# A decoder step on one core: which queue issues the sample's cache pages, when the mixer's output weights are converted, and where the attention output is split

## The chip, the cores and the metric

The kernel runs on one core of a Trainium2 chip. The metric is device time in microseconds (us) of one execution, the median of several runs; lower is better. The engines are TensorE (PE in the rows, its weight loads PEld), VectorE (DVE), ScalarE (ACT), GpSimd (POOL) and SyncE (SP). SP and POOL issue the transfers here, each from a queue of its own that works in order. Every engine takes its instructions in the order of the program.

## The reference

One layer of a hybrid decoder step for a prompt of 1024 tokens and a sample of 8 sequences with 4 new tokens each. A half-step SwiGLU block, a mixer, and a second half-step SwiGLU block follow each other, each under RMS norm and a modulation by the conditioning vector. The mixer:

```
n = modulated(x, g_mix, 1)
c_q, c_kv, k_pe, u, v, g_a, g_b = split_in(n @ w_in)
...
o_lat = attend(q_lat, q_pe, kv, k_pe)              # prompt: causal; sample: over the paged cache
o_a = einsum('bshc,chv->bshv', o_lat, w_uv)
v_n = layer_norm(gelu(v), ln_v_g, ln_v_b)
o_b = spatial_gating(gelu(u), v_n, w_s, b_s, chunk_len)
merged = sigmoid(g_a) * (o_a @ w_pa) + sigmoid(g_b) * (o_b @ w_pb)
x = x + gate[:, 1] * (merged @ w_o)
```

For the sample, `attend` reads 32 pages of 128 rows for each of 8 sequences through `page_table`: once for the scores (latent and rope part of each key row) and once for the values.

## The kernel before

Every fp32 product is made of three passes (`mm3`, L324 to L326): each operand is split into a rounded part (`whi`, by a cast on ACT, L186 or L330) and the remainder (`wlo`, by a subtraction on VectorE, L187 or L331). `conv_to` (L172 on) does that for the weights, in the order in which they were planned; `use(i, la)` asks for operand i and converts `la` operands ahead of it. It also brings the weights in through SP (`dma_to`, L163 and L161), some ahead of their conversion. Output weights w_o have one step more: POOL multiplies them by the gate first (`wg`, L184).

The prompt is worked in two halves of 512 tokens. After the first SwiGLU block and the projections of queries and keys, the mixer attends (about 905 to 1113 us) and then runs `post` for the one half (to about 1399) and the other (to about 1690). `post` splits the attention output `oaT` into OA (four casts, four subtractions), then takes v's rows (`rows_b` over four operands), u's rows, and five rounds p = 0 to 4. A round takes, for f = 0 and 1, the gates ga and gb (24 matmuls each), the output product `down` of the round before (with the two w_o operands, f = 0 only), and the merge weights pab, which meet OA and OB. In the plan of a round the operands stand in the order ga0, gb0, o0, o1, pab0, ga1, gb1, pab1. `ev_v`, a generator that is stepped between the matmuls, turns v's rows into normalised ones: four gelus on ACT, then squares, then VectorE's scaling.

The sample's attention (`s_attn`) is a generator too, stepped between the prompt's matmuls from about 891 to 1360. It works on four sequences at a time (g = 0, then 1). For g it makes 16 steps of scores: step r needs two pages of each of the four sequences (tiles pk, eight pages; `load_pk` asks for those of step r + 1 when step r is due; the matmuls of L1589 go through the four sequences first). Then follow eight groups of values (matmuls of L1635): each takes four tiles nat, one for each of the chunks c, with one page of each sequence, and asks for chunk c + 4 when chunk c has been used. A page is one transfer of 144 KB (pk) or 128 KB (nat), whose address comes from the page table, so its issue takes a few register instructions (L1546) ahead of the transfer (L1547). In both loads the pages alternate between SP and POOL. The pages are issued where the generator asks for them, so they share SP's queue with the weights, the x rows (L1078) and the stores, and POOL's with wg, the parts of norms that POOL does (L518, L519), and the product xT (L565). Tiles come from a pool of 46 slots (`u`); a load waits until its slot's former reader is done.

Of the kernel before, what the change touches and what calls it, by code (L numbers as in the profile page):

```python
# [9 lines left out]
FR = mybir.dt.float32r  # L10
# [6 lines left out]
P = 128  # L17
# [70 lines left out]
class Step:  # L88
# [1219 lines left out]

    def post(self, e, hf, nT, after=None, on=lambda what, p=0: None):
        nc = self.nc  # L1310
        OA = []
        for kt in range(4):
            w = self.u([P, 2, 512], FR, name="oa")
            self.split(w[:, 0], w[:, 1], self.oaT[kt // 2][hf][:, kt % 2])
            OA.append(w)

        vn = [self.u([P, 4, 256], F32, name="vn") for _ in range(2)]
        ub = [self.u([P, 4, 256], F32, name="ub") for _ in range(2)]
# [23 lines left out]
        def ev_u(ps):  # L1342
            for t in range(4):
                for g in range(2):
                    nc.scalar.activation(out=ub[g][:, t], in_=ps[t][:, 256 * g:256 * g + 256], func=AF.Gelu_apprx_tanh)
# [11 lines left out]
        fv.step()  # L1357
        self.fillers.append(fv)
        on("v")
        ps = [self.psb() for _ in range(3)] + [self.psa()]  # L1360
        ev_u(self.rows_b(e["u"], nT, ps))
        fv.finish()
# [22 lines left out]
        for p in range(5):  # L1385
            d = e["pairs"][p]
            if p < 4:
                hcur = []
                for f in range(2):
                    sg = []  # L1390
                    sgt = self.u([P, 2, 512], F32, name="sg")
                    for n in ("ga", "gb"):
                        ps = self.psa()
                        hi, lo = self.use(d["%s%d" % (n, f)], 2 if n == "gb" and f == 0 and p else 1)
                        for k in range(8):
                            x = nT[k]
                            self.mm3(ps, (hi[:, k, :], lo[:, k, :]), (x[:, 0], x[:, 1]), k == 0, k == 7)
                            if k % 2:
                                self.tick(1.3)
                        t = sgt[:, len(sg)]  # L1400
                        nc.scalar.activation(out=t, in_=ps, func=AF.Sigmoid)
                        sg.append(t)
                        if p == 0 and f == 0:
                            (mix if n == "ga" else mix_T)()
# [3 lines left out]
                    hi, lo = self.use(d["pab%d" % f], 2 if p == 3 and f else 1)  # L1408
                    if f == 0:
                        on("m", p)  # L1410
                    for n, X in ((0, OA), (1, OB)):
                        ps = self.psa()
# [7 lines left out]
                    w = self.u([P, 2, 512], FR, name="mg")  # L1420
# [128 lines left out]
    def s_attn(self):  # L1549

        nc, a = self.nc, self.a
# [7 lines left out]
        def load_pk(g, r, bs=(0, 1, 2, 3)):  # L1559
            if g > 1 or r > 15:  # L1560
                return
            for b in bs:
                t = self.u([96, 2, 3, P], F32, name="pk")
                for i in range(2):
                    self.page(t[:, i], "kvp", "o r c k -> r (o c) k", 4 * g + b, 2 * r + i, (nc.sync, nc.gpsimd)[i])
                pk[g, r, b] = t

        def load_nat(g, i):
            if (g, i) in nat or g > 1 or i > 31:
                return  # L1570
            t = self.u([P, 4, 256], F32, name="nat")
            for b in range(4):
                self.page(t[:, b], "kvn", "o k c -> k (o c)", 4 * g + b, i, (nc.sync, nc.gpsimd)[b % 2])
            nat[g, i] = t

        for g in range(2):
            if g == 0:
                load_pk(g, 0)
# [25 lines left out]
            for i in range(4):  # L1604
                load_nat(g, i)
# [16 lines left out]
            for i4 in range(8):  # L1622
                ps = self.pss()
                for i in range(4):
                    c = 4 * i4 + i
                    nc.tensor.transpose(ps[:, P * i:P * i + P], pt[c // 8][:, P * (c % 8):P * (c % 8) + P], self.idt)
                w = self.u([P, 4, P])
# [3 lines left out]
                for i in range(4):  # L1631
                    c = 4 * i4 + i
                    t = nat.pop((g, c))
# [36 lines left out]
        oa = self.s("sqn", [P, P], F32, 1)  # L1670
# [540 lines left out]
```

## Time and profile before

| | |
|---|---|
| median of 3 runs | 2395.5 us (2390.06 to 2398.54) |
| profiled execution | 2394.01 us |
| its span, first to last instruction | 2392.4 us |
| granted TensorE clock, mean | 0.987 |
| TensorE busy | 2294.7 us (96%) |
| VectorE, ACT, POOL busy | 57%, 34%, 36% |

The span is the time between the first and the last instruction of the profiled execution; 1.6 us of its time lie around it. A row of the timeline holds instructions of one form that follow each other on one engine, merged: start, length, engine, line, operation, tiles, count, and in brackets the idle time ahead of the row with what ended it. SPq and POOLq are the queues of SP and POOL on which transfers are issued; the length of such a row is that of the issue, not of the transfer.

### The profile page before, as it was taken

The numbers are of one execution on the slowest core, as the hardware profiler recorded it, in microseconds if no ns is written. First come the engines' busy times: TensorE is split into PE (matmuls) and PEld (weight loads), VectorE is DVE, ScalarE is ACT, GpSimd is POOL, SyncE is SP. The second block draws the span as 40 slices with busy tenths as digits, with TensorE's granted clock in tenths as the row PEclk, the third lists the DMA queues.
The fourth block names the chain that finished last, engine by engine and source line by source line (L and its number), as shares of the span: only waits on it lengthen the run. The fifth ranks groups of instructions, "written<-read, shape, count | busy, mean of one in ns | idle before, by whom it ended". The sixth has DMA issues, their size and how long they took to land.

```text
span 2392.4 us, 37074 instructions
## 1 busy us (share of the span) xinstructions
PE 2294.7 (96%) x12989; PEld 1750.0 (73%) x12989; DVE 1372.9 (57%) x1897; ACT 819.4 (34%) x1411; POOL 858.0 (36%) x822
## 2 busy tenths in 40 slices
PE   6999999998998999999999999999899999999998
PEld 4678787876776775556677777777677878877876
DVE  3766666663556555674344455445666666666557
ACT  4322222323334244553332243222532223233433
POOL 1364556450125123243223310011156565552125
PEclk9899999999999999999999999999999999999999
DMA  6244444459855237568877725542144444358643
GB/s 264 84 144 139 158 137 150 154 182 383 328 184 184 110 80 220 173 183 227 226 212 217 234 77 194 186 139 83 63 151 151 144 150 152 135 184 305 239 155 142
DMA packets 192516, 420.10 MB, mean 176 GB/s; under 512 B 21981, under 2 KB 80298, under 8 KB 192330
## 3 DMA queue, kind: packets, MB, share of 16 engines
q1 hardware_dynamic: 179242, 381.01, 46.7%
q0 software_dynamic: 12800, 36.19, 5.4%
q8 instruction: 103, 1.69, 0.3%
q14 instruction: 83, 0.68, 0.1%
q10 hardware_dynamic: 288, 0.52, 0.1%
HBM read 337.31 MB, written 78.23 MB: 174 GB/s over the span
## 4 chain that ended last, share of the span: by engine, by line
PE 77%; issue 6%; DMA 5%; DVE 5%; ACT 3%; POOL 2%; POOLq 1%; SPq 1%; DVEq 0%; ACTq 0%
PE psa L324 15%; PE psa L325 15%; PE psa L326 15%; PE psb L324 7%; PE psb L325 7%; PE psb L326 6%; PE pss L622 3%; DVE wlo L187 1%; PE pss L1589 1%; POOLq L1546 1%; PE psa L1211 1%; PE psa L441 1%; DMA nat<-in_kvn 1%; DMA w<-in_w1d 1%; DMA wada<-in_w_ada 1%
## 5 line engine op out<-in xcount | busy, mean ns | idle before, releaser
L187 DVE TENSOR_TENSOR wlo<-w,whi 128x1024 fp32r<-128x1024 f32 (+1 forms) x273 | 304.3, 1153 | 163.5 <-ACT whi L186 138.0
L186 ACT CAST whi<-w 128x1024 fp32r<-128x1024 f32 (+1 forms) x273 | 243.5, 927 | 208.9 <-PE psb L325 61.1
L326 PE MATMUL psa<-xT,ws 128*128 128x512 f32 x800 | 311.7, 390 | 2.0 <-DVE ws L331 2.0
L324 PE MATMUL psa<-xT,ws 128*128 128x512 f32 x800 | 313.2, 391 | 0.0
L325 PE MATMUL psa<-xT,ws 128*128 128x512 f32 x800 | 311.2, 389 | 0.0
L331 DVE TENSOR_TENSOR ws<-wsum,ws 128x512 fp32r<-128x512 f32 x160 | 170.5, 1065 | 28.8 <-ACT ws L330 28.8
L869 POOL TENSOR_TENSOR h<-hf,h 128x512 f32<-128x512 f32 x60 | 97.6, 1627 | 235.7 <-issue 191.0
L326 PEld LDWEIGHTS psa<-xT,ws 128*128 128x128 f32 x800 | 150.1, 188 | 34.3 <-DVE ws L331 2.8
L325 PEld LDWEIGHTS psa<-xT,ws 128*128 128x128 f32 x800 | 150.3, 188 | 30.6
L324 PEld LDWEIGHTS psa<-xT,ws 128*128 128x128 f32 x800 | 150.2, 188 | 30.4
L324 PE MATMUL psa<-xT,whi 128*128 128x512 f32 x384 | 160.1, 417 | 1.6 <-ACT xT L742 1.6
L325 PE MATMUL psa<-xT,whi 128*128 128x512 f32 x384 | 153.0, 398 | 0.0
L326 PE MATMUL psa<-xT,wlo 128*128 128x512 f32 x384 | 152.5, 397 | 0.0
L325 PE MATMUL psa<-wlo,whi 128*128 128x512 f32 x308 | 122.3, 397 | 9.4 <-DVE wlo L187 9.4
L331 DVE TENSOR_TENSOR ws<-w,ws 128x512 fp32r<-128x512 f32 x120 | 111.4, 928 | 33.9 <-ACT ws L330 33.9
L324 PE MATMUL psa<-whi 128*128 128x512 f32 x308 | 123.0, 399 | 6.2 <-ACT whi L186 6.2
L324 PE MATMUL psb<-xT,ws 128*128 128x512 f32 x320 | 127.1, 397 | 0.0
L325 PE MATMUL psb<-xT,ws 128*128 128x512 f32 x320 | 125.1, 391 | 0.0
L326 PE MATMUL psb<-xT,ws 128*128 128x512 f32 x320 | 124.6, 389 | 0.0
L324 PE MATMUL psb<-whi 128*128 128x512 f32 x308 | 122.5, 398 | 0.0
L326 PE MATMUL psa<-whi,wlo 128*128 128x512 f32 x308 | 121.6, 395 | 0.0
L325 PE MATMUL psb<-wlo,whi 128*128 128x512 f32 x308 | 121.2, 393 | 0.0
(397 smaller groups left out, 4820.2 us busy)
## 6 DMA issues: line engine op xcount, KB each, us to landing
wada<-in_w_ada SPq DMA_DIRECT2D x72, 512.0 KB
x<-x SPq DMA_DIRECT2D x40, 512.0 KB
pk<-in_kvp SPq DMA_DIRECT2D x128, 144.0 KB
pk<-in_kvp POOLq DMA_DIRECT2D x128, 144.0 KB, 3.8
w<-w1h SPq DMA_DIRECT2D x35, 512.0 KB
w<-w2h SPq DMA_DIRECT2D x35, 512.0 KB
nat<-in_kvn SPq DMA_DIRECT2D x128, 128.0 KB
nat<-in_kvn POOLq DMA_DIRECT2D x128, 128.0 KB, 3.0
```

What stands on the lines that cost most here:

```text
L186: self.nc.scalar.copy(hv(w.hi), src)
L187: self.nc.vector.tensor_tensor(out=hv(w.lo), in0=src, in1=hv(w.hi), op=ALU.subtract)
L324: nc.tensor.matmul(out, sh, mh, start=first, stop=False, skip_group_check=cont)
L325: nc.tensor.matmul(out, sh, ml, start=False, stop=False, skip_group_check=cont)
L326: nc.tensor.matmul(out, sl, mh, start=False, stop=last, skip_group_check=cont)
L331: self.nc.vector.tensor_tensor(out=lo, in0=src, in1=hi, op=ALU.subtract)
L441: nc.tensor.matmul(ps[32 * k:32 * k + 32, 256 * qq:256 * qq + 256], self.sc[:, 4 * kh + k, :], t[:, k, :], start=(kh == 0), stop=(kh == 1))
L622: self.nc.tensor.matmul(ps[32 * j:32 * j + 32, cols], st[:, k, :], mv, start=(k < 4), stop=(k >= nk - 4))
L869: nc.gpsimd.tensor_tensor(out=g, in0=t, in1=g, op=ALU.mult)
L1211: nc.tensor.matmul(ps[:, c:c + n], q, K[:, c:c + n], start=True, stop=not diag)
L1546: v = eng.value_load(self.pt[0:1, 32 * b + i:32 * b + i + 1], min_val=0, max_val=self.a[name].shape[0] - 1)
L1589: nc.tensor.matmul(ps[32 * b:32 * b + 32, 0:256], self.sqT[:, ch, 4 * g + b, :], ts[b][:, :, ch, :], start=(ch == 0), stop=(ch == 2))
```

## The change

Three edits. In `post` the split of OA moves from the head to the place behind v's rows and the first step of `ev_v`. In the rounds p = 1 to 3, `use` of ga0 (not only of gb0) converts two operands ahead, so that o0 is converted at ga0 and o1 at gb0, where both were converted at gb0. In `load_pk` both pages of the first of the four sequences are issued by SP; in `load_nat` two of the 16 pages of four chunks go from POOL to SP (sequence 3 in the first chunk, sequence 1 in the third, sequences counted from 0). SP issues five of eight pk pages and ten of sixteen nat pages, POOL the rest: 128 and 128 pk pages become 160 and 96, and so do the nat pages.

```
     def post(self, e, hf, nT, after=None, on=lambda what, p=0: None):
         nc = self.nc
-        OA = []
-        for kt in range(4):
-            w = self.u([P, 2, 512], FR, name="oa")
-            self.split(w[:, 0], w[:, 1], self.oaT[kt // 2][hf][:, kt % 2])
-            OA.append(w)
...
         fv.step()
         self.fillers.append(fv)
         on("v")
+        OA = []
+        for kt in range(4):
+            w = self.u([P, 2, 512], FR, name="oa")
+            self.split(w[:, 0], w[:, 1], self.oaT[kt // 2][hf][:, kt % 2])
+            OA.append(w)
...
-                        hi, lo = self.use(d["%s%d" % (n, f)], 2 if n == "gb" and f == 0 and p else 1)
+                        hi, lo = self.use(d["%s%d" % (n, f)], 2 if f == 0 and p else 1)
...
-                    self.page(t[:, i], "kvp", "o r c k -> r (o c) k", 4 * g + b, 2 * r + i, (nc.sync, nc.gpsimd)[i])
+                    self.page(t[:, i], "kvp", "o r c k -> r (o c) k", 4 * g + b, 2 * r + i, (nc.sync, nc.gpsimd)[i and b > 0])
...
-                self.page(t[:, b], "kvn", "o k c -> k (o c)", 4 * g + b, i, (nc.sync, nc.gpsimd)[b % 2])
+                self.page(t[:, b], "kvn", "o k c -> k (o c)", 4 * g + b, i, (nc.sync, nc.gpsimd)[b % 2 and b + i % 4 != 3])
```

The order of TensorE's instructions is the same in both programs. What stands in a row on the others, at three places:

SP's queue in the first half of `post`, at round p = 3, ahead of the load of the first of its two w_o operands (`in_w_o`; `sx` holds the page table), the difference:

```order
+L1546 TENSOR_LOAD sx
+L1546 ISA x2
+L1547 ISA
+L1547 DMA nat<-in_kvn 128x256
 L163 DMA w<-in_w_o 128x1024
+L1546 TENSOR_LOAD sx
```

A page that POOL issued before now stands directly ahead of the load, and another directly behind it; each of the batches of eight pages between the weight loads has become one of ten.

POOL's queue at round p = 2 of the first half, the difference around the first of the two products of w_o with the gate:

```order
 L1547 DMA nat<-in_kvn 128x256
+L184 TENSOR_TENSOR wg<-w,gb 128x1024
+L1546 TENSOR_LOAD sx
+L1546 ISA x2
+L1547 ISA
+L1547 DMA nat<-in_kvn 128x256
```

Both products stood behind one batch of eight pages; now the first stands ahead of a batch of six and the second behind it.

ACT at the start of `post` for the second half, where L558 ends the norm ahead of it, `whi` are the casts of v's and u's operands and `gv` the gelus, before:

```order
L558 ACTIVATE hf<-psa,mod 128x512 x8
L330 CAST oa<-oaT 128x512 x4
L186 CAST whi<-w 128x1024 x4
L1325 ACT_TABLE_LOAD
L1325 ACTIVATE gv,ln<-psa 128x512 x4
L186 CAST whi<-w 128x1024
L1697 ACTIVATE sgv,sln<-pss 32x512
```

and now:

```order
L558 ACTIVATE hf<-psa,mod 128x512 x8
L186 CAST whi<-w 128x1024 x4
L1320 ACT_TABLE_LOAD
L1320 ACTIVATE gv,ln<-psa 128x512 x4
L330 CAST oa<-oaT 128x512 x4
L186 CAST whi<-w 128x1024
L1697 ACTIVATE sgv,sln<-pss 32x512
```

The four casts of OA went from ahead of v's operands to behind the gelus, ahead of the cast of u's second operand; in the first half they move past the same instructions.

## Rows read from the trace of the kernel before

**Rows 1.** The page's first part: busy time, share of the span and count of instructions of each engine.
```profile
PE 2294.7 (96%) x12989; PEld 1750.0 (73%) x12989; DVE 1372.9 (57%) x1897; ACT 819.4 (34%) x1411; POOL 858.0 (36%) x822
```
**Rows 2.** The list of TensorE's waits over the whole span: who waited for whom, us in total, times, longest us.
```profile
PE pss L1635 <- DMA nat<-in_kvn: 3.8, 3, 1.8
PE pss L1589 <- DMA pk<-in_kvp: 2.9, 4, 1.4
...
PE psb L325 <- DVE wlo L187: 2.1, 2, 1.3
...
PE psb L324 <- ACT whi L186: 0.8, 1, 0.8
```
**Rows 3.** The timeline of SP's queue from 904 to 1000 us: the store of pe_prompt, the pages of score steps 1 to 15 of the first four sequences, and the first pages of the values.
```profile
904.59 0.40 SPq L1136 DMA_DIRECT2D out_pe_prompt<-peo  x1
905.84 76.61 SPq L1547 DMA_DIRECT2D pk<-in_kvp  x60
986.34 8.36 SPq L1547 DMA_DIRECT2D nat<-in_kvn  x8
```
**Rows 4.** The chain of work that ended last, from 900 to 990 us: start, length, what; for a transfer the length is from its issue to the release of what waited for it.
```profile
905.84 2.86 DMA pk<-in_kvp
```
**Rows 5.** The same queue's timeline cut at 910 us.
```profile
905.84 4.16 SPq L1547 DMA_DIRECT2D pk<-in_kvp  x4
```
**Rows 6.** The page's last part: issues of a line, KB each, and for POOL the median us from issue to landing.
```profile
pk<-in_kvp POOLq DMA_DIRECT2D x128, 144.0 KB, 3.8
```
**Rows 7.** TensorE's timeline at score steps 1 (two rows, 23 of its 24 matmuls recorded), 12 and 13.
```profile
910.17 0.63 PE L1589 MATMUL pss<-pk,sqT 96*32 96x256 f32 x4
911.72 1.65 PE L1589 MATMUL pss<-pk,sqT 96*32 96x256 f32 x19 [0.92 <-DMA pk<-in_kvp]
...
972.06 1.50 PE L1589 MATMUL pss<-pk,sqT 96*32 96x256 f32 x24
975.23 2.46 PE L1589 MATMUL pss<-pk,sqT 96*32 96x256 f32 x24
```
**Rows 8.** TensorE's timeline from 1060 to 1105 us: its waits for ACT's hf and, in the last two groups of values, for pages.
```profile
1074.74 0.44 PE L1239 MATMUL psb<-cst,p 128*128 128x128 f32 x2 [2.12 <-ACT hf L558]
...
1091.84 1.37 PE L1635 MATMUL pss<-nat,u 128*32 128x256 f32 x6 [0.88 <-DMA nat<-in_kvn]
...
1103.69 0.62 PE L1635 MATMUL pss<-nat,u 128*32 128x256 f32 x2 [1.75 <-DMA nat<-in_kvn]
```
**Rows 9.** POOL's timeline from 1064 to 1080 us.
```profile
1067.32 0.55 POOL L1547 DMA_DIRECT2D nat<-in_kvn  x1 [0.79 <-PE psb L1239]
1068.51 0.55 POOL L1547 DMA_DIRECT2D nat<-in_kvn  x1 [0.65 <-issue]
1069.08 1.28 POOL L565 TENSOR_TENSOR xT<-hf,xT 128x512 fp32r<-128x512 f32 x1
```
**Rows 10.** SP's queue from 1010 to 1100 us: the pages of chunks 4 to 31 of the first four sequences.
```profile
1016.18 75.95 SPq L1547 DMA_DIRECT2D nat<-in_kvn  x56
```
**Rows 11.** The start of `post` for the first half: ACT (OA, then the cast of u[1]), VectorE (its remainder), TensorE (its first use, and a wait for a page).
```profile
1114.05 2.18 ACT L330 CAST oa<-oaT 128x512 fp32r<-128x512 f32 x4
...
1145.28 1.06 ACT L186 CAST whi<-w 128x1024 fp32r<-128x1024 f32 x1
...
1146.37 1.23 DVE L187 TENSOR_TENSOR wlo<-w,whi 128x1024 fp32r<-128x1024 f32 x1 [5.10 <-ACT whi L186]
...
1147.90 0.40 PE L324 MATMUL psb<-whi,xT 128*128 128x512 f32 x1
...
1161.28 1.48 PE L1589 MATMUL pss<-pk,sqT 96*32 96x256 f32 x18 [1.45 <-DMA pk<-in_kvp]
```
**Rows 12.** Round p = 2 of the first half: POOL's two products, and TensorE in `down`.
```profile
1281.56 4.76 POOL L184 TENSOR_TENSOR wg<-w,gb 128x1024 f32<-128x1024 f32 x2
...
1287.47 0.49 PE L325 MATMUL psb<-wlo,mg 128*128 128x512 f32 x1 [1.30 <-DVE wlo L187]
```
**Rows 13.** SP's queue from 1284 to 1346 us, round p = 3 coming: the batches of pages, the loads of x and of w_o's second operand (loads of gates and merge weights between them left out).
```profile
1288.68 9.09 SPq L1547 DMA_DIRECT2D nat<-in_kvn  x8
...
1300.12 8.77 SPq L1547 DMA_DIRECT2D nat<-in_kvn  x8
...
1313.18 8.35 SPq L1547 DMA_DIRECT2D nat<-in_kvn  x8
1321.71 0.34 SPq L163 DMA_DIRECT2D w<-in_w_o  x1
1322.96 8.42 SPq L1547 DMA_DIRECT2D nat<-in_kvn  x8
1331.48 2.08 SPq L1078 DMA_DIRECT2D x<-x  x4
1333.73 0.50 SPq L163 DMA_DIRECT2D w<-in_w_o  x1
```
**Rows 14.** The chain of work that ended last, from 1280 to 1360 us.
```profile
1333.73 8.93 DMA w<-in_w_o
```
**Rows 15.** TensorE's timeline from 1342 to 1362 us, in `down` of round p = 3 and in the last group of values.
```profile
1346.31 0.51 PE L324 MATMUL psb<-whi,mg 128*128 128x512 f32 x1 [0.85 <-ACT whi L186]
1347.57 0.51 PE L325 MATMUL psb<-wlo,mg 128*128 128x512 f32 x1 [0.76 <-DVE wlo L187]
1357.25 0.62 PE L1635 MATMUL pss<-nat,u 128*32 128x256 f32 x2 [1.13 <-DMA nat<-in_kvn]
```
**Rows 16.** The start of `post` for the second half: ACT (OA), VectorE (OA's remainders, the copy of G), TensorE (v[1]'s remainder, then G).
```profile
1399.47 2.17 ACT L330 CAST oa<-oaT 128x512 fp32r<-128x512 f32 x4
...
1402.33 3.12 DVE L331 TENSOR_TENSOR oa<-oaT,oa 128x512 fp32r<-128x512 f32 x4
...
1426.31 0.69 DVE L1685 COPY G<-pss 128x512 f32<-128x512 f32 x1 [0.36 <-PE pss L622]
...
1406.63 0.50 PE L325 MATMUL psa<-wlo,xT 128*128 128x512 f32 x1 [1.40 <-DVE wlo L187]
...
1427.05 1.05 PE L1433 MATMUL pss<-G,cst 128*32 128x512 f32 x2 [0.81 <-DVE G L1685]
```

## The prediction

> **What bounds the kernel now.** I read the page first. TensorE is busy for 96% of the span [rows 1], so the change can win only what TensorE idles, and can lose whatever it adds to that. The list of TensorE's waits then gives the kinds of idle time that the three edits can touch: the sample's pages (nat and pk) and the operands of the output weights (wlo, whi) [rows 2]. All together are some 10 us of 2392.4, and each wait is worth only its own length. So the second question decides: what do the engines that are handed work have to spare? SyncE (SP) is handed 64 pages, POOL gives up 64. An issuing engine's rows tell that, stage by stage: how many pages stand in how many microseconds, against how many could.
>
> **The price of a page.** Eight pages without a wait between them take 8.36 us on SP's queue [rows 3], the last one's own row 0.34, so (8.36 - 0.34) / 7 = 1.146 us from page to page; this is time of the issuing queue, and it does not overlap. How long after its issue a page lands: one that SP issued 905.84 us into the span released its waiter 2.86 us later [rows 4], the fourth of that stretch was issued at 910.00 - 0.32 = 909.68 [rows 5]; POOL's pk pages have a median of 3.8 [rows 6]. TensorE waited for that fourth page until 911.72 [rows 7], 2.04 us. For SP I take 2.4, between its two.
>
> **Page edit, first pk stage (scores of sequences 0 to 3).** Fifteen steps are loaded in this stage; each took four pages from SP and takes five now. SP starts at 905.84, behind the store of pe_prompt (which waits for VectorE's peo), and its 60 pages spread over 76.61 us [rows 3]. Without waits they would take 59 x 1.146 + 0.34 = 68.0, so SP has 8.6 us to spare, and 15 added pages cost 15 x 1.146 = 17.2. The difference must come out at TensorE. Step 1 already waited 0.92 us for SP's fourth page [rows 7]; the fifth comes 1.15 later. Step 13 binds most: its fifth page is SP's 65th of this stretch, issued at 905.84 + 64 x 1.146 = 979.2 and landed at 981.6. TensorE began that step at 975.23, needs the page at its fourth matmul (975.5), and spent 2.46 instead of 1.50 us on the step, so it would have waited until about 976.4 anyway [rows 7]. That makes 5.2 to 6.1 us. I take **+5.8**. Low end: landing after 2.04, need at 976.4, +4.8. High end: in the first step the extra page also stands ahead of the w_v loads on SP; if these set peo, all of SP's pages start 1.15 later: landing after 2.86 as well, 979.2 + 1.15 + 2.86 = 983.2 against 975.5, +7.7. POOL's relief here is worth nothing by itself, since the steps would wait for SP.
>
> **Page edit, first nat stage.** Here POOL is the late one: TensorE waited 0.88 and 1.75 us for nat pages, and 2.12 for ACT's hf [rows 8], behind which stands POOL's xT, begun at 1069.08, right after the last of a row of pages that POOL issues 1.19 us apart [rows 9]. POOL issues six pages per group now instead of eight, 2 x 1.19 = 2.4 us less in each group. The first two waits go, and about half of the 2.12 (POOL reaches xT sooner, VectorE's cast still stands ahead): 0.88 + 1.75 + 1.1 = **-3.7**; bounds -1 (the pages moved to SP take their place) and -5.4. SP's 56 pages spread over 75.95 us from 1016.18 [rows 10]; 70 take 69 x 1.146 + 0.34 = 79.4. Started 5.8 late, the last one lands at 1016.2 + 5.8 + 79.1 + 2.4 = 1103.5; TensorE, 5.8 - 3.7 = 2.1 late by then, wants it near 1103.7 - 1.75 + 2.1 = 1104.0. This closes with half a microsecond to spare.
>
> **OA splits, first half.** Four casts on ACT (2.18 us) and four subtractions on VectorE leave the head of the stage [rows 11], where TensorE waited for none of them: no gain. They now stand behind v's four gelus and ahead of the conversion of u[1]. That conversion's cast began at 1145.28 and its wlo at 1146.37, 1.23 long; TensorE used the first of it at 1147.90 [rows 11]. Cast and wlo go back 2.18, so wlo is ready at 1146.37 + 1.23 + 2.18 = 1149.8, and TensorE wants it one matmul after 1147.90: +1.7. The wait for POOL's pages at 1161.28 (1.45), which are held behind the squares of ev_v, has 1.7 us more time and one page in four fewer: it goes. Net **+0.4**, bounds -1.4 and +1.9.
>
> **Output weights one operand sooner, half A.** At p=2 both wg multiplies of POOL ran in one piece, 4.76 us, from 1281.56, behind eight pages; TensorE waited 1.30 for wlo [rows 12]. Now the first wg stands six pages ahead of the second: the 1.30 goes. No instruction is added; on ACT the same cast, some 1.06 us, now stands ahead of a copy of probabilities (u) and a sigmoid. I cost that at nothing, as TensorE reads u some matmuls later; where wg's data come late, ACT waits with it, and the copy behind it too, up to a wg multiply and a cast (2.4 + 1.06). At p=3 that can be so, but any such wait lies inside the one that follows. For at p=3 it is another resource. SP's rows there run with hardly a gap from 1288.68 to 1333.73: four batches of eight pages took 9.09, 8.77, 8.35 and 8.42 us, where 8.36 is the time without waits [rows 13], so 1.1 us are spare. Behind them stand four loads of x and then w_o's second half, issued at 1333.73, which released POOL 8.93 us later [rows 14]; wg, cast and wlo followed, and TensorE waited 0.85 and 0.76 [rows 15]. Each of these four batches has two pages more: 8 x 1.146 = 9.2, less 1.1, less 0.7 because the first batch may start that much earlier (its first page waited for p=2's late wlo). The w_o load moves back 7.4 us and everything behind it with it: TensorE resumes 7.4 later than before, whatever it gained at p=2 (that gain is used up by the longer wait, so it is not counted again): **+7.4**, bounds +5.5 (the load lands faster, now that x is ahead by the same distance but POOL's pages are fewer) and +8.5. The last nat wait of this half, 1.13 us for a page of POOL [rows 15], goes: **-1.1**, or 0 if SP's ten pages of that group take its place.
>
> **Half B.** No pages here. w_o is converted in time already, so its edit costs and gains nothing. The OA splits leave the start: ACT's casts from 1399.47 and VectorE's subtractions from 1402.33 stood ahead of v[1]'s wlo, for which TensorE waited 1.40 [rows 16]: -1.4. They then stand behind the gelus and ahead of u[1]; VectorE's copy of G at 1426.31, for which TensorE already waits 0.81, stands behind u[1]'s wlo, and that behind ACT's four casts (2.17) and the subtractions that follow them. Copy and reader go back by about as much as the casts take, less the 0.36 for which VectorE stood idle before the copy: 2.17 - 0.36 = +1.8. Net **+0.4**, bounds -1.4 and +2.
>
> **Sum.** 5.8 - 3.7 + 0.4 + 7.4 - 1.1 + 0.4 = +9.2 us. The profiled execution took 2394.0, so 2403.2; the median of the runs shown is 1.5 higher (2395.5), which makes **2404.7**.
>
> **The rivals.**
> *Faster.* A page costs SP less than its row says once it has nothing to wait for, and lands sooner than POOL's: 2.04 to 2.86 against a median of 3.8 [rows 4 to 7]. Then SP keeps up everywhere and only gains are left: -0.9 (step 1) - 3.7 + 0.4 - 1.3 - 1.1 + 0.4 = -6.2, and up to 1.6 more at p=3: 2387.7 to 2389.3. For it: the two longest waits for nat pages, 1.75 and 1.13, and the longest for pk, 1.45, are for POOL's. Against it: 8.36 us for eight pages is measured in stretches in which SP waits for nothing. The Trainium skill, "DMA: Bandwidth & Descriptors", section "SWDGE vs HWDGE vs iDMA", has it this way: transfers issued by SP or ACT have their descriptors made by hardware and are faster to set up than GpSimd's, so plain transfers belong on SP. By that rule alone the page edit would be a gain and the sum -6.2. The rows agree on the landing, but in the issue a page costs SP 1.146 and POOL 1.19, nearly the same, and it is the issue that adds up.
> *No change.* Only one of SP's two delays comes out. If SP's pages of the first pk stage are hidden (less time of its own per page there, or TensorE held by others), 9.2 - 5.8 = +3.4: 2398.9. If the w_o load is not delayed (x or w_o released sooner), 9.2 - 7.4 - 1.3 = +0.5: 2396.0. It decides at SP's spare time: 8.6 us in the one place, 1.1 in the other.
> *Slower still.* SP also falls behind in the first nat stage, where the sum closed with 0.5 us to spare, and the w_v loads delay the start: +3 to +6, 2408 to 2410.
> *The edit does less than it says:* TensorE's order is the same in both programs, the tables of SP and POOL do change, so I give this nothing.
>
> **How the numbers follow.** Forecast 0.40 (own range 2400 to 2408), no change 0.28, faster 0.22, slower still 0.10. A measurement of this kernel can tell some 0.3%, 7.2 us, from no change: 2388.3 and 2402.7. The forecast lies above that bound by less than 2 us, so a sixth of its chance falls within it. Faster 0.22, within 0.28 + 0.06 = 0.34, slower 0.34 + 0.10 = 0.44. The range reaches from the faster case, whose far end it leaves out, to the upper case's end: 2388 to 2410.
>
> **What would show it.** In the changed profile SP's 75 pages of the first pk stage run without gaps to about 991, and steps 12 to 15 of the scores wait for SP's pages, several microseconds in all; POOL's waits at the end of the first nat stage are gone; the w_o load at p=3 is issued 7 us later relative to TensorE's work before it, with one wait of 6 to 9 us for whi and wlo there; TensorE's 1.30 at p=2 and 1.40 at v[1] of half B are gone, and G's copy is waited for 2.7 us. I am wrong if SP issues pages closer than 1.1 us, if x and w_o are not behind the batches, or if pages that land sooner move TensorE's other waits too.

## The result and the profile after

The changed kernel takes 2418.0 us (median of 4 runs, 2416.4 to 2421.3) against 2393.8 (4 runs, 2390.1 to 2398.5): ratio 1.0101 [1.0086, 1.0116], slower by 24.2 us, where 2404.7 was forecast. The profiled execution took 2417.9, its span is 2416.2, 23.8 longer than before. The page's first part, against [rows 1]: POOL has 64 instructions less (its pages), TensorE the same ones.

```profile
PE 2302.5 (95%) x12989; PEld 1752.1 (73%) x12989; DVE 1378.7 (57%) x1897; ACT 820.2 (34%) x1411; POOL 827.3 (34%) x758
```

The list of TensorE's waits, against [rows 2]: nat fell from 3.8 to 1.7, but pk rose from 2.9 to 7.9 and whi from 0.8 to 7.6.

```profile
PE pss L1589 <- DMA pk<-in_kvp: 7.9, 11, 1.4
PE psb L324 <- ACT whi L186: 7.6, 2, 7.3
...
PE pss L1433 <- DVE G L1685: 2.4, 1, 2.4
...
PE psb L325 <- DVE wlo L187: 2.0, 3, 0.8
...
PE pss L1635 <- DMA nat<-in_kvn: 1.7, 4, 0.5
```

TensorE's instructions stand in the same order in both programs, so the start of the same matmul can be read in both timelines. The difference of the two is how far TensorE is behind; where it grows, time is lost (one profiled execution of each kernel; up to 880 us, ahead of the three edits, those of the runs below lie between 3.1 us ahead of the kernel before and 0.5 behind, so a long stretch can differ by a few microseconds without an edit):

| place | start before | start after | behind | of this stretch | forecast |
|---|---|---|---|---|---|
| ahead of the first score stage | 880.08 | 880.60 | 0.5 | | |
| end of that stage | 1000.41 | 1010.29 | 9.9 | +9.4 | +5.8 |
| after the first value stage | 1120.14 | 1126.18 | 6.0 | -3.9 | -3.7 |
| behind u[1] of half A | 1158.20 | 1165.91 | 7.7 | +1.7 | +1.7 |
| behind score step 5, second four sequences | 1178.20 | 1189.07 | 10.9 | +3.2 | -1.4 |
| behind p=2's `down` | 1304.12 | 1314.79 | 10.7 | -0.2 | 0 |
| p=3's `down`, ahead of its second operand | 1344.17 | 1358.39 | 14.2 | +3.6 | 0 |
| the same `down`, behind it | 1352.06 | 1374.56 | 22.5 | +8.3 | +7.4 |
| behind the last group of values | 1360.09 | 1380.84 | 20.8 | -1.8 | -1.1 |
| half B under way | 1449.10 | 1470.80 | 21.7 | +1.0 | +0.4 |
| last matmul | 2383.65 | 2404.62 | 21.0 | -0.7 | |
| end of the span | 2392.4 | 2416.2 | 23.8 | +2.8 | 0 |

**First score stage.** SP's timeline from 904 to 1010 us, against [rows 3], where 60 pages took 76.61:

```profile
906.35 87.81 SPq L1547 DMA_DIRECT2D pk<-in_kvp  x75
996.23 10.96 SPq L1547 DMA_DIRECT2D nat<-in_kvn  x10
```

SP runs without a gap, as forecast, at (87.81 - 0.34) / 74 = 1.182 us a page. TensorE's timeline at steps 13 and 14 (24 matmuls each), against [rows 7]: it waits there for pages, shortly each time, since it has already fallen back to SP's pace.

```profile
984.28 0.59 PE L1589 MATMUL pss<-pk,sqT 96*32 96x256 f32 x2 [0.16 <-DMA pk<-in_kvp]
985.39 1.46 PE L1589 MATMUL pss<-pk,sqT 96*32 96x256 f32 x18 [0.52 <-DMA pk<-in_kvp]
...
991.70 1.45 PE L1589 MATMUL pss<-pk,sqT 96*32 96x256 f32 x18 [0.33 <-DMA pk<-in_kvp]
```

**Score step 5 of the second four.** TensorE's timeline there, against [rows 11], and POOL's behind it. TensorE goes on some 3.5 us after POOL's issues of the two pages at 1165.55 and 1166.85; between 1160.94 and 1165.55 POOL issued nothing, and the profile names nothing that it waited for (`<-issue`).

```profile
1168.98 0.62 PE L1589 MATMUL pss<-pk,sqT 96*32 96x256 f32 x2 [1.45 <-DMA pk<-in_kvp]
1170.58 2.50 PE L1589 MATMUL pss<-pk,sqT 96*32 96x256 f32 x18 [0.97 <-DMA pk<-in_kvp]
```
```profile
1160.94 0.59 POOL L1547 DMA_DIRECT2D pk<-in_kvp  x1 [0.30 <-issue]
1165.55 0.51 POOL L1547 DMA_DIRECT2D pk<-in_kvp  x1 [4.01 <-issue]
1166.85 0.51 POOL L1547 DMA_DIRECT2D pk<-in_kvp  x1 [0.79 <-issue]
```

**Second value stage.** SP's timeline, from the batch of p=2 on, against [rows 13]:

```profile
1283.02 1.24 SPq L161 DMA_DIRECT2D w<-in_w_pab  x2
1288.27 11.03 SPq L1547 DMA_DIRECT2D nat<-in_kvn  x10
...
1303.02 11.19 SPq L1547 DMA_DIRECT2D nat<-in_kvn  x10
...
1316.44 10.51 SPq L1547 DMA_DIRECT2D nat<-in_kvn  x10
...
1330.52 11.02 SPq L1547 DMA_DIRECT2D nat<-in_kvn  x10
...
1342.87 10.62 SPq L1547 DMA_DIRECT2D nat<-in_kvn  x10
1353.59 1.84 SPq L1078 DMA_DIRECT2D x<-x  x4
1355.53 0.39 SPq L163 DMA_DIRECT2D w<-in_w_o  x1
```

From the batch at 1303.02 to the load of w_o it is 52.5 us, before (1288.68 to 1333.73) 45.1: 7.5 more, as forecast. But the batch itself stands 14.3 later than before, with TensorE 11.0 behind: 3.4 late, not 0.7 early. So the load is 21.8 - 11.0 = 10.8 late. TensorE's timeline: short waits for SP's pages in three groups of values (a row each of the first and the last), which put it 3.5 us back in all, and then the wait for whi, against [rows 15].

```profile
1316.80 0.62 PE L1635 MATMUL pss<-nat,u 128*32 128x256 f32 x4 [0.55 <-DMA nat<-in_kvn]
```
```profile
1343.32 0.62 PE L1635 MATMUL pss<-nat,u 128*32 128x256 f32 x4 [0.55 <-DMA nat<-in_kvn]
```
```profile
1366.97 0.80 PE L324 MATMUL psb<-whi,mg 128*128 128x512 f32 x1 [7.29 <-ACT whi L186]
1368.23 0.80 PE L325 MATMUL psb<-wlo,mg 128*128 128x512 f32 x1 [0.47 <-DVE wlo L187]
```

Stretches of the same profile (length; busy time and count of PE, PEld, DVE, ACT, POOL; granted clock, DMA share, GB/s). Behind the waits TensorE works at a lower granted clock: 0.56, 0.61, 0.50, where 0.50 is the lower of its two levels, 1.2 instead of 2.4 GHz. Before, all stretches from 1340 to 1365 us show 1.00.

```profile
945.00:950.00 5.00, 5.00 (x21) 3.02 (x14) 1.52 (x4) 0.45 (x2) 0.00 (x0) 0.56 0.48 135
...
1170.00:1174.00 4.00, 3.42 (x20) 1.69 (x21) 0.88 (x2) 0.43 (x2) 1.54 (x3) 0.61 0.68 205
...
1365.00:1370.00 5.00, 2.57 (x5) 1.77 (x6) 3.05 (x4) 2.47 (x3) 2.97 (x5) 0.50 0.86 240
```

### The profile page after: what moved, and what is told of

Same layout as the page of the kernel before. It is cut to its first block, busy times and chain, and to the rows that moved or that the text cites. A ratio compares the mean times of both kernels' runs of the same rounds, so it can differ in the third digit from the quotient of the medians.

```text
span 2416.2 us, 37026 instructions
## 1 busy us (share of the span) xinstructions
PE 2302.5 (95%) x12989; PEld 1752.1 (73%) x12989; DVE 1378.7 (57%) x1897; ACT 820.2 (34%) x1411; POOL 827.3 (34%) x758
## 4 chain that ended last, share of the span: by engine, by line
PE 78%; DVE 5%; DMA 5%; issue 4%; ACT 3%; POOL 2%; SPq 1%; POOLq 1%; DVEq 0%; ACTq 0%
PE psa L324 15%; PE psa L325 15%; PE psa L326 14%; PE psb L324 7%; PE psb L325 7%; PE psb L326 7%; PE pss L622 2%; PE psa L1211 2%; DMA wada<-in_w_ada 2%; PE pss L1589 2%; DVE wlo L187 1%; PE psb L1256 1%; PE psa L441 1%; DVE xT L746 1%; DMA pk<-in_kvp 1%
```

## Experiments

A change such as +8.1 us is the ratio to the kernel before, run beside it, taken of some 2395 us; the brackets hold the ratio's 95% interval, and 0.001 of it is 2.4 us. The tail is the time from the end of the last matmul to the end of the span, 8.3 us before.

**Each edit alone**, made in the kernel before.

```diff
e1_pk:   - 2 * r + i, (nc.sync, nc.gpsimd)[i])
         + 2 * r + i, (nc.sync, nc.gpsimd)[i and b > 0])
e2_nat:  - 4 * g + b, i, (nc.sync, nc.gpsimd)[b % 2])
         + 4 * g + b, i, (nc.sync, nc.gpsimd)[b % 2 and b + i % 4 != 3])
e3_oa:   the loop that splits OA moved from the head of post behind v's rows (on("v"))
e4_wo:   - 2 if n == "gb" and f == 0 and p else 1
         + 2 if f == 0 and p else 1
```

> The kernel before with one of the three edits alone: five of eight score pages (pk) on SP, three on POOL. Pace theory (SP's queue issues a page each 1.15 us and has 8.6 us to spare in the first score stage, 17.2 are added; waits there also let the granted clock fall): TensorE is 9 to 10 us late by the end of that stage, as in the changed kernel, of which some 3.4 us stand as a granted clock below 1.00 around 940 to 955 us; nothing in the second score stage, where SP waits for slots; total +8 to +10 us. Rival (tiles of the other two edits sit in later slots, and the pages wait for those): the score stage waits no more than before, total within 2 us of before.

Measured: 2402.0, 1.0034 [1.0020, 1.0049], +8.1. TensorE falls 8.6 behind in the first score stage, with the granted clock at 1.00 there: the debt to SP alone sets it. In the first value stage 3.4 come back: no page is waited for there, though the value pages stand on the queues as before (why is told under POOL's count). The last matmul is 4.3 late; the rest of the loss stands behind it, in the tail.

> The kernel before with the value pages (nat) alone moved: ten of sixteen on SP, six on POOL. Pace theory: the waits for POOL's pages at the end of the first value stage go (-3 to -4 us), in the second SP has about 1 us to spare between 1288 and 1334 us and is given eight pages, so the second w_o operand at p=3 is issued 8 us later and TensorE waits 8 to 10 us there instead of 1.6: total +3 to +6 us. Rival (the delay of w_o in the changed kernel comes from the slots that the w_o edit moves, not from the pages): w_o waits 2 to 4 us, total -3 to 0 us.

Measured: 2404.4, 1.0046 [1.0033, 1.0059], +11.0. At p=3 the wait for w_o is there, 9.21 + 0.47, and the first value stage gains 2.7; the tail adds 5.4.

> The kernel before with only the split of OA moved behind v's rows. Order theory (engines' queues alone): u[1] is waited for 1.5 us more, v[1] of the second half 1.4 less, G 1.7 more, the wait for POOL's page at score step 5 of the second four sequences stays near 1.45: total +1 to +2.5 us. Slot theory (OA's four tiles are taken later, so the pages of that step get slots that come free later): that step waits 2.4 us or more and the granted clock falls behind it as in the changed kernel, total +4 to +6 us.

Measured: 2403.6, 1.0035 [1.0019, 1.0052], +8.4, far over the working. The waits of u[1] (0.36 + 0.76) and of G (2.44) are as expected. In its profile (2406.4) TensorE also waits 1.12, 3.62 and 1.59 for POOL's pages at the end of the first value stage, ahead of the edit, where nothing in the program differs from the kernel before, and loses 8.9 us there (from 1090 to 1120 us); at score step 5 it waits 0.30 and 1.78 and loses 2.8.

> The kernel before with only w_o's first operand converted one operand sooner. Order theory: the wait of 1.30 us at p=2 shrinks to 0.7 or less, the waits at p=3 stay at 1.6 in all: total -0.5 to -1.5 us. Slot theory (the merge weights' load is asked for sooner and stands with its slot wait ahead of the pages of chunks 8 to 11, which start 5 us later than before): SP's batch of chunks 12 to 15 starts 2 to 4 us later, the second w_o load of p=3 with it, and TensorE waits 3 to 5 us at p=3: total +1 to +3 us.

Measured: 2391.0, 0.9989 [0.9976, 1.0001], -2.6: a small gain or none.

**Is the queue ahead of w_o the cause?** In f1 and f2 the load of w_o's second operand stands ahead of the four loads of x.

```diff
f1_nat_wofirst = e2_nat, f2_wo_wofirst = e4_wo, each with, ahead of x's loads:
+                    k.dma_to(e["pairs"][3]["ro"][1] + 1)
```

> The value pages moved (as e2_nat, +11 us), and the load of w_o's second operand for round 3 of the first half asked for ahead of the four loads of x instead of behind them. Queue theory (that load is late because SP's queue is late: eight more pages, then x's four issues of 0.5 us and their 2 MB ahead of it): it is issued 2 us sooner and lands 6 to 7 us sooner, the wait of 9 to 10 us shrinks to 2 to 4, total +3 to +5 us against the kernel before. Rival (the wait is made of something behind the load, POOL's product or a slot): the wait stays above 7, total +9 to +11 us.

Measured: 2403.2, 1.0047 [1.0031, 1.0064]. The load is issued at 1335.90 instead of 1342.62, and the wait is 2.90 instead of 9.21: shown for the wait. The total is that of e2_nat within its interval; of the 9.0 us in its profile 5.4 stand in the tail.

> The w_o edit alone (e4_wo, -2.6 us) with the same load ahead of x, pages as before. Queue theory: the waits of 1.3 and 0.8 us at round 3 go, total -4 to -5 us. Rival: the x rows, now later, are waited for by the norm of the second half, or nothing changes: total -2.6 or above.

Measured: 2389.4, 0.9976 [0.9967, 0.9986], -5.7: faster than both kernels. No wait for w_o's whi or wlo is left at p=3. SP's timeline:

```profile
1322.18 8.42 SPq L1547 DMA_DIRECT2D nat<-in_kvn  x8
1330.70 0.38 SPq L163 DMA_DIRECT2D w<-in_w_o  x1
1331.17 2.47 SPq L1078 DMA_DIRECT2D x<-x  x4
```

**Two controls.** The splits of OA behind u's rows too; and the mirror of e1_pk, with POOL taking the five pages.

```diff
f3_oa_late:   the loop that splits OA moved behind u's rows (fv.finish())
f4_pk_mirror: - (nc.sync, nc.gpsimd)[i])
              + (nc.sync, nc.gpsimd)[i or b == 0])
```

> The split of OA alone moved, but behind u's rows, where the casts of u are done, instead of ahead of u's second operand. Order theory (what OA's edit costs is that ACT and VectorE convert OA ahead of u[1] and of the copy of G): the waits at u[1] and the longer one at G do not come, the 1.4 us at v[1] of the second half go, total -0.5 to -2 us. Slot theory (OA's tiles taken later shift the slots of pages and weights): the pages of score step 5 still wait longer and the total is +3 us or more, as in e3_oa (+8.4).

Measured: 2396.3, 1.0005 [0.9996, 1.0015]. The longer waits of u[1] and G are gone with the place, as expected; the gain of 0.5 to 2 us does not show in the total.

> The mirror of e1_pk: of eight score pages three on SP and five on POOL. Pace theory (each queue issues a page in 1.15 to 1.27 us, and four per step of 5.5 us already fill it to 85 to 92%): POOL needs 6.0 to 6.3 us per step, falls behind more than SP did in e1_pk, total +10 to +16 us. Rival (only SP's queue is a bound, since it carries the stores and weights): total within 3 us of before.

Measured: 2408.1, 1.0057 [1.0040, 1.0075], +13.7. Its last matmul is 13.3 late, that of e1_pk 4.3. In the first score stage itself the two cost nearly the same, 10.0 and 8.6 us: there the even split before is at both queues' limit. Most of the difference comes later (e1 gets 3.4 back in the first value stage, f4 0.1), and in the total POOL is the worse one to burden. The rule of the Trainium skill that the prediction weighed ("DMA: Bandwidth & Descriptors", section "SWDGE vs HWDGE vs iDMA": plain transfers belong on SP or ACT) agrees with that order; a gain from moving them to SP no run shows (+8.1).

**The changed kernel with one thing put back** (g2, h1 to h4), **the pages the other way** (g1), **and f2 with one part of the page edit** (g3, g4).

```diff
g1_swap (from before): page edit of e1_pk, and - [b % 2] + [b % 2 or b == i % 4]
g2_after_no_oa:    the loop that splits OA at the head of post again
g3_wo_natfirst = f2 and [b % 2 and (g > 0 or b + i % 4 != 3)]
g4_wo_pksecond = f2 and [i and (g == 0 or b > 0)]
h1_after_wofirst:  + k.dma_to(e["pairs"][3]["ro"][1] + 1) ahead of x's loads
h2_after_pk_g0:    - [i and b > 0]  + [i and (g == 0 or b > 0)]
h3_after_nat_g1:   - [b % 2 and b + i % 4 != 3]
                   + [b % 2 and (g > 0 or b + i % 4 != 3)]
h4_after_no_wo:    - 2 if f == 0 and p else 1
                   + 2 if n == "gb" and f == 0 and p else 1
```

> Score pages as in e1_pk (five SP, three POOL) and value pages the other way (six SP, ten POOL of sixteen), so that POOL issues 256 pages in all, as in the kernel before. It tells what the time behind the last matmul hangs on: 8.3 us in every kernel with 256 pages on POOL, 13.8 with 224 (e1_pk, e2_nat, f1_nat_wofirst), 11.1 with 192 (the changed kernel), spent in POOL's DRAIN. Count theory: 8.3 us here. Rival (any departure from four and four costs it): 11 or more. Ahead of it POOL is the late one in the value stages and TensorE some 5 to 20 us later than before; the w_o waits of 1.6 us at round 3 go.

Measured: 2416.7, 1.0091 [1.0075, 1.0107], tail 8.3. POOL is late now: TensorE waits 5.7 for ACT's hf in the first value stage.

> The changed kernel with the split of OA back at the head. If the edits add up as they do alone (pk +8.1, nat +11.0, w_o -2.6, and the tail of 224 pages counted once at 192 pages instead of twice), TensorE ends 12 to 15 us later than before and the time is +14 to +18 us, with the wait for w_o at round 3 still 7 us or more. Rival (OA's delay only overlaps with later waits for pages and w_o, so taking it out gives nothing): +21 us or more.

Measured: 2418.7, 1.0095 [1.0077, 1.0114]: the changed kernel's time. In it the OA edit costs nothing that can be measured, and step 5 waits (0.99 and 0.72) without it.

> f2_wo_wofirst (-5.7 us) with ten of sixteen value pages on SP for the first four sequences only, where SP has time; POOL issues 240 pages. Ahead of the last matmul the waits for nat pages at the end of the first value stage go: -1.5 to -3 us. Behind it the count theory says something other than 8.3 us (it has no number for 240). Total -8 us if the tail stays, -2 to -4 if it grows to 11 to 14.

Measured: 2396.0, 1.0011 [1.0002, 1.0020], tail 8.3. The gain expected on top of f2 did not come: it is 7 to 8 us slower than f2.

> f2_wo_wofirst (-5.7 us) with five of eight score pages on SP for the second four sequences only, where SP waits for slots 27 us in all; POOL issues 240 pages. Pace theory: SP has the time, the wait for POOL's page at score step 5 of that stage shrinks by about 1.5 us with the granted clock's fall behind it, -1 to -3 us ahead of the last matmul; the tail is the same as in g3_wo_natfirst, since the count is the same. Rival (five pages per step on SP cost time in this stage too): +3 us or more.

Measured: 2392.3, 0.9994 [0.9984, 1.0003]. Neither part of the page edit adds to f2; both are slower than f2.

> The changed kernel with the load of w_o's second operand for round 3 ahead of the loads of x. Queue theory: the wait of 7.3 us there shrinks to 1 to 2 us and the fall of the granted clock behind it becomes shorter, total 5 to 8 us less than the changed kernel, +16 to +19 against the kernel before. Rival (the late pages of the last value groups take its place): +21 or more.

Measured: 2416.7, 1.0088 [1.0069, 1.0108]. The wait for whi falls from 7.29 to 1.19, and a new one stands eight us later, for VectorE's x, whose load now stands behind: the wait moved.

```profile
1362.86 0.49 PE L324 MATMUL psb<-whi,mg 128*128 128x512 f32 x1 [1.19 <-ACT whi L186]
1364.11 0.50 PE L325 MATMUL psb<-wlo,mg 128*128 128x512 f32 x1 [0.76 <-DVE wlo L187]
1371.36 0.80 PE L324 MATMUL psb<-whi,mg 128*128 128x512 f32 x1 [4.70 <-DVE x L733]
```

What a run lies under the changed kernel is the difference of two medians, here and below; by the two ratios it is 9.6 us for h2, 8.9 for h3 and 7.9 for h4, each uncertain by some 6 us. So the stretches of the profiles say where it comes from.

> The changed kernel with the score pages of the first four sequences four and four again. Pace theory: TensorE is no longer 9 us late at the end of the first score stage, but part of that comes back as waits for value pages at the end of the next stage, which starts sooner: total 5 to 9 us less than the changed kernel, +15 to +19. Rival (the delay of this stage is all given back by the next one): +22 or more. The tail for 208 pages on POOL has not been seen.

Measured: 2408.6, 1.0061 [1.0042, 1.0079], 9.4 under the changed kernel. TensorE loses 0.1 instead of 9.4 in the first score stage, and step 5 does not wait.

> The changed kernel with the value pages of the second four sequences eight and eight again. Pace theory: SP's batches of ten become eight there, the waits for nat pages between 1316 and 1343 us (1.5 us) and for w_o (7.3) fall to less than 3 us together, total 8 to 12 us less than the changed kernel, +12 to +16. Rival (w_o is late for the merge weights' load that the w_o edit has moved ahead of the pages): the wait stays above 4 us, +19 or more. The tail is that of h2_after_pk_g0, since the count is the same.

Measured: 2410.9, 1.0064 [1.0043, 1.0085], 7.2 under it. From 1280 to 1400 TensorE gains 0.4 where it loses 9.7 in the changed kernel: with eight pages a group on SP there is no loss.

> The changed kernel without the w_o edit. If that edit makes the load of w_o later (the pages of chunks 8 to 11 start 5 us later behind the merge weights' load): 2 to 4 us less than the changed kernel, +20 to +22. If it is worth what it is worth alone (-2.6): +25 to +28.

Measured: 2411.9, 1.0068 [1.0048, 1.0088], 6.1 under it. In its profiled execution (2415.8) TensorE loses 7.0 from 1280 to 1360 us, 2.8 less than in the changed kernel. SP's timeline shows what the edit does: without it the batch stands ahead of the loads of w_pab.

```profile
1276.60 0.84 SPq L163 DMA_DIRECT2D w<-in_w_o  x2
1280.62 10.90 SPq L1547 DMA_DIRECT2D nat<-in_kvn  x10
1291.70 1.23 SPq L161 DMA_DIRECT2D w<-in_w_pab  x2
```

TensorE is 8.6 behind there and 11.0 in the changed kernel; 1288.27 - 11.0 against 1280.62 - 8.6 is 5.3 us later. In the changed kernel w_pab waited 3.5 us for a slot, and the batch behind it another 3.5. The batch after it, the first of the four ahead of w_o's load, starts 3.4 to 3.5 us late against TensorE in all six kernels with the w_o edit and ten pages (after, g2, h1, h2, i1, i2) and 0.2 to 0.7 early in the three with ten pages and without the edit (e2, f1, h4): an edit that is no loss alone costs here.

**POOL's count.** In the traces of all the kernels so far POOL's 129th DMA stands 3.46 to 3.48 us between the register instructions ahead of it and its issue, whatever it carries and whenever it comes: at 1079.7 before, at 1165.5 in the changed kernel, where it is the page of step 5, at 1094.0 in h2. Others stand 0.52 us when they wait for nothing. And POOL's closing drain, the instruction with which it ends the program, lasts the longer, the more DMAs POOL has issued since the last multiple of 128.

The stall also explains waits for pages in the first value stage. POOL's timeline in the kernel before, and in e1, which issues the same pages there but has the 129th DMA behind the stage, at 1107.8:

```profile
1075.38 1.26 POOL L565 TENSOR_TENSOR xT<-hf,xT 128x512 fp32r<-128x512 f32 x1 [5.03 <-DVE xT L564]
1079.65 0.56 POOL L1547 DMA_DIRECT2D nat<-in_kvn  x1 [3.01 <-PE pss L1635]
```
```profile
1083.27 1.26 POOL L565 TENSOR_TENSOR xT<-hf,xT 128x512 fp32r<-128x512 f32 x1 [5.03 <-DVE xT L564]
1084.60 0.57 POOL L1547 DMA_DIRECT2D nat<-in_kvn  x1
```

The row names a matmul of TensorE's, but the page stood as long as the 129th DMA of the others. TensorE's wait for hf ahead of it is the same, 2.12 and 2.13. Behind it the kernel before waits 0.88 and 1.75 for pages [rows 8] and e1 not at all. The five other kernels with an even split in that stage and the 129th DMA at 1076 to 1079 (e3, e4, f2, f3, g4) wait 1.7 to 6.3 us for pages there.

A second stall of the same kind, which the count of 128 does not give, stands at POOL's 249th DMA in the kernel before, e3, e4, f2 and f3 (3.42 us), at the 250th in f4 (3.45) and at the 246th in g1, g4 and i1 (3.35); the kernels with 208 to 240 DMAs end ahead of it. Of those with 256, g3 has a wait of 6.4 us at its 249th that could hide it, and i2 (below), whose last 48 are tiny, shows none. Two more runs move the count alone.

```diff
+        xd = k.s("xd", [16, 64])
+            nc.gpsimd.dma_start(out=xd[:, j:j + 1], in_=a["g_qkv"].to_broadcast([16, 512])[:, j:j + 1])
i1_after_58_early: 29 such behind each rows_ckv
i2_after_48_late:  12 such at each "p" of half B
```

> The changed kernel with 58 tiny loads (16 x 1 elements, into a tile that nothing reads) added to POOL's queue in two idle stretches of POOL between 820 and 876 us. Theory (POOL's DMAs are counted, and the 129th stands some 3.5 us): the 129th is then the page that was the 71st, near 1026 us, the page of score step 5 of the second four sequences is issued 3.5 us sooner and its waits of 1.45 and 0.97 us go, with the clock's fall behind them (3.2 us of TensorE's shift); 266 DMAs are 10 past 256, so POOL's closing drain is under 3.2 us and the tail behind the last matmul 8.3 instead of 11.15: 2418.0 - 3.2 - 2.8 = 2412. Rival (the 3.48 us belong to that page, its slot or its place in the program): the gap and the two waits stay near 1165, the tail stays 11.15, 2418.

Measured: 2414.8, 1.0085 [1.0056, 1.0114]. The 129th is the page at 1026.56; POOL stood 25 us ahead of it, waiting for a slot, so that a stall of its own can't be told apart. The page of step 5 is issued without a gap. From 1120 to 1200 TensorE loses 0.6 instead of 4.8. TensorE's timeline at step 5, and POOL's row of the 129th:

```profile
1165.06 1.48 PE L1589 MATMUL pss<-pk,sqT 96*32 96x256 f32 x18 [0.48 <-DMA pk<-in_kvp]
```
```profile
1026.56 0.55 POOL L1547 DMA_DIRECT2D nat<-in_kvn  x1 [25.43 <-PE psb L1239]
```

> The changed kernel with 48 of the same tiny loads on POOL's queue in the second half of the mixer, behind its last page, twelve for each round. Theory (the drain lasts as long as the DMAs since the last multiple of 128 make it): 256 DMAs, drain about 2 us, tail 8.3 to 8.6 instead of 11.15, score step 5 unchanged: 2418.0 - 2.7 = 2415. Rival (the drain's length is one of the pages, their bytes or their place): the tail stays 11.15, 2418; if small loads count by their size, between the two.

Measured: 2413.6, 1.0089 [1.0063, 1.0116]. POOL's timeline shows the gap in its old place, and TensorE waits 1.11 and 1.22 in step 5; the tail is 8.6.

```profile
1158.73 0.59 POOL L1547 DMA_DIRECT2D pk<-in_kvp  x1 [0.30 <-issue]
1163.33 0.52 POOL L1547 DMA_DIRECT2D pk<-in_kvp  x1 [4.00 <-issue]
```

| kernels | POOL's DMAs | past a multiple of 128 | drain, us | last matmul to end, us |
|---|---|---|---|---|
| i1 | 266 | 10 | 2.98 | 8.3 |
| before, e3, e4, f2, f3, g1 | 272 | 16 | 3.22 (g1 3.47) | 8.3 |
| f4 | 304 | 48 | 5.75 | 9.1 |
| after, g2, h1, h4 | 208 | 80 | 7.80 | 11.2 |
| h2, h3 | 224 | 96 | 9.10 | 12.5 |
| e1, e2, f1 | 240 | 112 | 10.41 | 13.8 |
| g3, g4, i2 | 256 | 0 | 1.83 to 2.16 | 8.3 to 8.6 |

Both theories hold for this stall and for the drain: with 58 DMAs ahead the stall leaves the page of step 5, with 48 behind it stays, and the drain goes by the count (up to about 5 us it is hidden behind the last stores: 5.75 add 0.8 to the tail, 10.41 add 5.5). The two totals lie 3.2 and 4.4 us under the changed kernel's, which their intervals can't tell from it.

## Why the prediction was wrong

The direction was right, and so was the mechanism where it was priced: SP has nothing to spare, in two places. The size was not, 9.2 us against 24.2 (23.8 in the profiled executions). Of the 14.6 us between, the first score stage makes 3.6, score step 5 4.6, round p=3 3.8 and the end 2.8; two of these four were terms sized wrongly, the other two a behaviour of POOL that stands in no term. By the steps of the prediction:

- **First pk stage, +5.8, measured +9.4: mis-sized.** The price of a page was taken from a batch of values (1.146). SP's 65th page was issued at 982.4, not 979.2: 0.5 by a later start, most of the rest by the pace (64 x 0.036 = 2.3). It released TensorE 3.0 us later, not 2.4. A row for this very kind of page was at hand, four pages in 4.16 us [rows 5], or (4.16 - 0.34) / 3 = 1.27 each. e1 and h2 show the term alone: +8.6 in TensorE, and 9.4 less in the total when it is undone.
- **First nat stage, -3.7, measured -3.9: the number right, the reason only in part.** The wait for hf fell from 2.12 to 1.62, by 0.5 and not by 1.1. The waits for pages (0.88 and 1.75, now 0.26) were put down to POOL's share of the pages. But e1 moves no value page and is rid of them too: in the kernel before they follow POOL's 129th DMA. That the sum agrees is luck.
- **OA splits, first half: one part right, one failed.** u[1] cost 1.7, as worked out. "It goes" was said of the wait of step 5; it came to 2.4 us and a clock of 0.61 behind, +3.2 instead of -1.4. What held that page longer was POOL's 129th DMA, which 64 pages less on POOL had moved from the first value stage to there. i1 and i2 show it, and so do all the kernels with five pages of eight on SP at that step: with the 129th DMA there (after, g2, h1, h3, h4, i2) the stretch costs 1.3 to 4.4 us, with it elsewhere (e1, g1, g4, h2, i1) it gains 0.9 to 1.7. So without the stall the forecast of -1.4 holds. The stall was in no part of the prediction.
- **Output weights, p=2: right** in the sum (-0.2). The wait of 1.30 went, and one of 0.76 stands in its place.
- **Output weights, p=3, +7.4 and -1.1, measured +3.6 and +8.3 less 1.8: the failed step is "less 0.7 because the first batch may start that much earlier".** It starts 3.4 later, since the edit moved the loads of w_pab, with their wait for a slot, ahead of a batch that stands on the same queue. Without the edit it does start 0.2 to 0.7 earlier (e2, f1, h4), and in h4 the load of w_o is 1349.90 - 1333.73 - 8.6 = 7.6 late, as forecast; with it 10.8. (In e2 it is 10.0 late: x's four loads take 4.2 us there and not 2.1.) The prediction counted that "no instruction is added" and followed the edit on POOL and ACT, not on SP. The pages themselves took 7.5 more, 8.1 in the forecast.
- **The clock behind a wait.** The prediction priced a wait at its own length. At p=3 the two waits are 6.2 us longer than the two before (7.29 + 0.47 - 0.85 - 0.76), but the stretch lost 8.3: 2.1 stand in matmuls at 0.50 to 0.77 of the clock.
- **Half B, +0.4, measured +1.0:** v[1]'s 1.40 went, G's wait is 2.44, as worked out; 0.6 more follow it.
- **The end, nothing in the sum, measured +2.8: not seen.** 208 DMAs instead of 272 leave 80 past a multiple of 128, and the drain outlasts the last stores.

Two slips of the working are small: 1.7 less 1.45 is +0.25, not +0.4, and four batches of 34.63 us against 4 x 8.36 leave 1.2 us, not 1.1.

Of the rivals none gives the time. "Slower still" (2408 to 2410) put its loss where none came, in the first value stage. "No change" needed one of SP's two delays to stay away; both came. "Faster" fell: SP's pages took 1.18 us in a stretch where SP waits for nothing.

The edits do not add up: alone +8.1, +11.0, +8.4 and -2.6 make 24.9, which agrees with 24.2 by chance only. OA costs nothing measurable inside (g2), the output weights cost inside and not alone, and the alone-runs of the page edits hold 5.4 us of tail each, the changed kernel 2.8.

Open: why e3_oa is 8.4 slower alone. In its profile most of the loss stands behind POOL's 129th DMA, in the first value stage ahead of the edit, and f3_oa_late (+1.2) shows such waits too (1.47 and 2.96); why they are 1.7 us in one kernel and 6.3 in another is not known. Open too what POOL does in the 3.47 us of its 129th DMA, and why the second stall comes 117 to 121 DMAs later: the count is shown for the first, the cause behind it not. f2 with the 129th DMA moved ahead of the value stage was not tried.

## What to carry to other kernels

Before work is moved to a queue, count stage by stage what that queue has to spare, at the price of just this kind of transfer, and list everything that an edit's operands load on that queue too: a conversion made one step sooner takes its loads past whatever stands there. An even split that looks idle on average can be at both queues' limit, as here, where one page in eight moved either way costs. Price a wait with what TensorE loses behind it. After a change in POOL's DMA count look for its stalls in another place, and before a gain is put down to moved work, look whether a stall has left the stage.

## What the runs showed of the hardware

- The 129th DMA that POOL issues stood 3.46 to 3.48 us in 19 of 20 traces; in the other (i1) it is hidden in a wait of 25 us for a slot. A second stall of 3.35 to 3.45 us stood at the 246th, 249th or 250th DMA in nine traces, and not at the 257th (0.52 us in the kernel before).
- POOL's closing drain lasted between 1.8 and 10.4 us by the count of POOL's DMAs past a multiple of 128, 0.073 us for each from 48 to 112, (10.41 - 5.75) / 64. It lengthened the program above about 5 us. Loads of 16 elements count as pages of 128 KB do (i1, i2).
- The granted clock did not follow the length of a single wait alone. Behind waits of 2.12, 2.44, 7.29 and 9.21 us a stretch at or near half of it came every time; behind 1.62 in the changed kernel (at 1084.5) it was 0.66, behind 1.75 in the kernel before (at 1103.7) 1.00; behind two waits shortly after each other 0.61 (1.45 and 0.97) or 1.00 (1.11 and 1.22, i2). What decides is open.
